# Part of the value projections of a hybrid decoder layer by Strassen's scheme, in one stage at the kernel's start

## The chip, the cores and the metric

The kernel runs on one core of a Trainium2 chip. The metric is the device time of one execution in microseconds: 1766.05 us before the change, the median of 3 runs (1765.07 to 1771.58). The profile is of one further execution, with the hardware's own record of what each engine did. PE is the matrix engine (TensorE), with its weight loads as PEld; DVE is the vector engine, ACT the scalar engine, POOL is GpSimd, and SP is the engine whose queue issues most of the DMAs.

## What is computed

One decoder layer on 1024 tokens of width 1024, all in fp32. Cut to what matters:

```python
h = rms_norm(x, pre_mix_g)                       # one scale per token, one gain per channel
proj = h @ w_in                                  # 8192 columns
qa, ka, va, qb, kb, vb, gates = split(proj)      # va: 512 columns, vb: 3 groups of 512
oa = diff_attention(rope(qa), rope(ka), va)      # 4 heads, causal, two softmaxes each
ob = merge of 3 dilated groups(rope(qb), rope(kb), vb)   # 4 heads per group
mix = (sigmoid(g_a) * (norm(oa) @ w_a_out) + sigmoid(g_b) * (ob @ w_b_out)) @ w_mix_out
x = x + rms_norm(mix);  x = x + rms_norm(conv_glu(rms_norm(x)))
```

The change touches `va` (512 columns) and the first group of `vb` (512 columns): two matrix products of the 1024 x 1024 normed input with 1024 x 512 weights.

## The kernel before

Every matrix product is made three times over. An fp32 operand is split into a high part, rounded to the format that PE multiplies in one pass, and a low part, the rest; a product is high x high + high x low + low x high (`mm3`, lines 146 to 149). A split (`split`, line 142) is one copy on ACT and one subtraction on DVE (lines 143 and 140). One PE matmul holds a 128 x 128 block still and streams up to 512 columns past it.

The input stands transposed in SBUF, as high and low parts `xh` and `xl`: 8 blocks of 128 channels, 1024 tokens each. The per-token norm factor `rstd` isn't in it. It is multiplied in behind each product: for values as a scale of the evacuation, for q and k through the rope tables, for gates through `rstd_row`. So products can start before the norm is known.

The stages, in order:

1. **First gates** (lines 318 to 376). The transposed input is loaded block by block, scaled by the gain and split; the first three gate units (128 columns each) run over it as the blocks arrive, on six PSUM banks. Behind that come the sums of squares of x (line 383), `rstd`, and the sine and cosine tables (`tables`, line 289), which are stored to DRAM and loaded in the layouts that the heads want (`load_tabs`).
2. **Start** (lines 674 to 676): `START_GATES` = 2 more gate units, the values of heads 0 and 1 of the first attention (`proj_v(VA, ...)`), the q and k of head 0 (`proj_a`).
3. **First attention**, heads 0 to 3. Each head has eight score blocks whose chain goes PE, DVE, ACT, DVE, PE, and beside them projections for later work as filler: `A_FILLS` (line 50) names them for each head. "p" and "P" are the q and k of the next head (8 units), "g" a gate (4 units), "v" and "w" the two halves of the values of heads 2 and 3 (4 units each), "V" the values of the second attention's group 0, first pair (8 units). A unit is 12 matmuls of 512 columns or 24 of 256. `interleave` (line 257) spreads them in step with the blocks.
4. **Second attention**, 12 steps of (pair, group, head), with the q and k of the next step (8 units) and half of the values of the next group (4 units) as filler (lines 862 to 873).
5. Output projections and the mixing matrix, then the gated MLP, whose two large products are already made by Strassen's scheme, with seven products of half-size blocks.

A values projection (`proj_v`, lines 429 to 466) covers 256 columns: it loads two weight units of 512 columns, splits them, and for each of eight token tiles runs 8 x 3 matmuls in which the input block is held and 256 weight columns stream (lines 438 to 440). Values of the first attention and of group 0 (dilation 1) go straight from PSUM to their split tiles (lines 448, 449). Those of dilated groups go through DRAM, where they are reordered (line 453).

The order of the program's text is not the order on the engines. A planner (line 1465) simulates all engines and places each instruction on its engine when its operands are ready, earlier text first; `tc.high_priority` moves some work ahead. What it decides is fixed in the program: each engine then runs its instructions in that order. Raw weights pass through `load_raw` (line 118), a two-buffer tag of the pool `rt`; split weights through six pairs of buffers (`slot_w`, line 114); PSUM has eight banks (`acc` 3, `pt` 2, `ps_s` 2, `ps_o` 1).

Of the kernel before, what the change touches and what calls it, by code (L numbers as in the profile page):

```python
# [24 lines left out]
P = 128  # L25
# [33 lines left out]
def plan():  # L59

    order = [("t", GT + i * P) for i in FIRST_GATES]
    for pair in range(2):
        for h in (2 * pair, 2 * pair + 1):
            order += [("t", QA + h * P), ("t", KA + h * P)]
            if h % 2 == 0:
                order += [("v", VA + pair * 256, i) for i in range(2)]
    for pair in range(2):
        for g in range(BG):
            order += [("v", VB + g * 512 + pair * 256, i) for i in range(2)]
            for h in (2 * pair, 2 * pair + 1):  # L70
                order += [("t", QB + g * 512 + h * P), ("t", KB + g * 512 + h * P)]
# [17 lines left out]
def trunk(ctx: ExitStack, tc: tile.TileContext, a, out):  # L89
# [28 lines left out]
    def load_raw(src):  # L118
        raw = raws_in[-1].tile([P, 512], F32, tag="raw", name="raw")
        dma(raw, src)  # L120
# [72 lines left out]
    v_d = dram.tile([4, S, 256], F32, name="v_d")  # L193
    gt_d = dram.tile([2 * KC, P, S], F32, name="gt_d")
# [82 lines left out]
    tabs = open_pool(attn, "tabs", side="right")  # L277
    rstd_row = tabs.tile([P, S], F32, name="rstd_row")
    slots = open_pool(attn, "slots", side="right")
    st_a = ExitStack()  # L280

# [7 lines left out]
    def tables(sin, cos, tmp):  # L289

        pos = tmp.tile([P, S], I32, tag="kk", name="pos")
        ang = tmp.tile([P, S], F32, tag="ang", name="ang")
        kk = tmp.tile([P, S], F32, tag="kk", name="kk")
        dma(pos, a["positions"].partition_broadcast(P))
        nc.vector.tensor_copy(ang, pos)
        nc.vector.tensor_scalar(ang, ang, cols[:, 0:1], None, op0=ALU.mult)
        for dst, off in ((sin, 0.0), (cos, 0.25)):
# [7 lines left out]
        nc.scalar.activation(sin, sin, AF.Sin)  # L305
        nc.scalar.activation(cos, cos, AF.Sin, bias=half_pi)
# [11 lines left out]
    with ExitStack() as st0:  # L318
        prep = open_pool(st0, "prep")
        ssx = prep.tile([P, 8], F32, name="ssx")  # L320
        raws = [prep.tile([P, 1024], F32, tag=f"raw{n}", name="raw") for n in range(len(FIRST_GATES))]
        first = [[Joined(t) for t in zip(*(slot_w() for _ in range(2)))] for _ in FIRST_GATES]
        xts = {}
# [9 lines left out]
        def load_x(k, parts=1):  # L333
            xts[k] = prep.tile([P, S], F32, tag="xt", name="xt", bufs=3)
# [10 lines left out]


# [9 lines left out]
        load_x(1)  # L356
        split_x(1)
# [3 lines left out]
        for k in range(2, KC):  # L361
            load_x(k)
            split_x(k)
        dma(cols, a["cols"])
# [3 lines left out]
        for k in range(KC):  # L368
            w = slice(k * P, (k + 1) * P)
            for n, ps in enumerate(pss):  # L370
                (wh, wl), sl = first[n // 2], halves()[n % 2]
                mm3(ps, wh[:, w], wl[:, w], xh[:, k, sl], xl[:, k, sl], k == 0, k == KC - 1)
# [5 lines left out]

        for m in range(8):
            t = prep.tile([P, D], F32, tag="xt", name="xn", bufs=3)  # L380
            dma(t, a["x"][m * P : (m + 1) * P, :])
            sq = prep.tile([P, D], F32, tag="kk", name="sq")
            nc.scalar.activation(sq, t, AF.Square, accum_out=ssx[:, m : m + 1])
        with tc.high_priority(offset=60):
            nc.vector.tensor_copy(rstd, rsqrt(ssx, D, prep, "rx"))
            spread = rstd_row.rearrange("p (m q) -> p m q", q=P)
            nc.vector.tensor_copy(spread, rstd.unsqueeze(2).to_broadcast([P, 8, P]))
        tab = [prep.tile([P, S], F32, tag="xt", name=n, bufs=3) for n in ("sin", "cos")]
        tables(*tab, prep)
        neg = prep.tile([P, S], F32, tag="xt", name="neg", bufs=3)  # L390
        for half, sl in enumerate(halves()):
            row = psum(F32, pt, "pt")
            for b in range(4):
                nc.tensor.transpose(row[:, b * P : (b + 1) * P], spread[:, half * 4 + b], ident)
            nc.scalar.activation(rstd_row[:, sl], row, AF.Copy)
# [1073 lines left out]
```

## Time and profile before

| | |
|---|---|
| median of 3 runs | 1766.05 us (1765.07 to 1771.58) |
| profiled execution: its time, its span | 1767.12 us, 1765.3 us |
| PE busy | 1721.8 us, 98% of the span, 8754 matmuls |
| DVE busy | 1329.9 us, 75% |
| ACT busy | 865.3 us, 49% |
| first gates end on PE, about | 43.4 us |
| start stage on PE: two gates, values, q and k of head 0 | 43.4 to about 118 us |
| mean granted clock of PE | 0.990 |

The span runs from the program's first instruction to its last. Busy time of an engine is the time in which at least one of its instructions is under way. The granted clock is the share of its full clock that PE was given. In a group of instructions the columns are line, engine, operation, what is written and read, shape and count, then busy us and the mean ns of one, then the engine's idle time just before them and what ended it. PE's matmuls overlap, so their mean is longer than the distance from one to the next.

### The profile page before, as it was taken

The page shows a single profiled execution, that of the slowest core. Times are in us where ns is not written, and L with a number is a line of the kernel's source. Part 1 is how long each engine was busy: PE and PEld are TensorE (multiplying, and loading weights), DVE is VectorE, ACT ScalarE, POOL GpSimd, SP SyncE. Part 2 cuts the span into 40 slices and gives each one's busy share as a digit, 9 for nine tenths or more (in the row PEclk, how much of TensorE's full clock was granted, in tenths as well). Part 3 has the DMA queues.
Part 4 walks back from the last instruction along what each step waited for, and adds up shares of the span by engine and source line. Part 5 has one row for each costly group of instructions (what it writes and reads, how often), then busy time and mean ns, then how long its engine had stood idle before and what let it go on. Part 6 is the DMA issues. An engine that isn't in the chain of part 4 may idle for free.

```text
span 1765.3 us, 24106 instructions
## 1 busy us (share of the span) xinstructions
PE 1721.8 (98%) x8754; PEld 1459.4 (83%) x8754; DVE 1329.9 (75%) x2612; ACT 865.3 (49%) x1585; POOL 51.6 (3%) x78
## 2 busy tenths in 40 slices
PE   9999999999999999999999999999999999999997
PEld 7987788789888888888877878878888888888886
DVE  4667786776556667565665867799999999789978
ACT  6375464644455645465652533364444444355452
POOL 0000000000000000000000410300000000000000
PEclk9999999999999999999999999999999999999999
DMA  8411112211121335221376533023222222196624
GB/s 271 162 60 42 54 55 72 78 55 59 56 86 60 102 97 156 75 88 55 126 254 222 166 131 108 37 72 107 90 78 95 78 78 96 60 342 216 206 77 155
DMA packets 100407, 197.61 MB, mean 112 GB/s; under 512 B 16368, under 2 KB 23216, under 8 KB 100288
## 3 DMA queue, kind: packets, MB, share of 16 engines
q1 hardware_dynamic: 92192, 185.06, 31.4%
q10 hardware_dynamic: 8096, 11.01, 1.7%
q8 instruction: 68, 1.11, 0.3%
q14 instruction: 51, 0.42, 0.1%
HBM read 152.37 MB, written 43.66 MB: 111 GB/s over the span
## 4 chain that ended last, share of the span: by engine, by line
PE 78%; DVE 9%; DMA 7%; issue 3%; ACT 3%; SPq 1%; POOL 0%; DVEq 0%; ACTq 0%
PE acc L148 15%; PE acc L147 15%; PE acc L149 15%; PE acc L438 3%; PE acc L440 3%; PE acc L439 3%; PE acc L1301 3%; PE acc L1300 3%; PE acc L1302 3%; PE acc L990 2%; PE acc L991 2%; PE acc L989 2%; PE o L484 2%; PE pt L472 1%; DMA og<-og_d 1%
## 5 line engine op out<-in xcount | busy, mean ns | idle before, releaser
L147 PE MATMUL acc<-xh,whi 128*128 128x512 f32 x744 | 296.3, 399 | 4.7 <-DVE t L421 2.6
L148 PE MATMUL acc<-xh,wlo 128*128 128x512 f32 x744 | 296.9, 399 | 1.4 <-DVE wlo L140 1.4
L149 PE MATMUL acc<-xl,whi 128*128 128x512 f32 x744 | 294.6, 398 | 0.0
L143 ACT ACTIVATE whi<-raw 128x512 fp32r<-128x512 f32 (+1 forms) x258 | 158.8, 624 | 208.5 <-PE acc L149 125.2
L140 DVE TENSOR_TENSOR wlo<-raw,whi 128x512 fp32r<-128x512 f32 (+1 forms) x255 | 185.0, 732 | 47.3 <-ACT whi L143 45.8
L147 PEld LDWEIGHTS acc<-xh,whi 128*128 128x128 f32 x744 | 140.6, 189 | 33.6 <-ACT xh L342 3.2
L148 PEld LDWEIGHTS acc<-xh,wlo 128*128 128x128 f32 x744 | 140.8, 189 | 29.2 <-DVE wlo L140 1.6
L149 PEld LDWEIGHTS acc<-xl,whi 128*128 128x128 f32 x744 | 141.2, 190 | 28.7
L147 PE MATMUL acc<-mh,whi 128*128 128x512 f32 x400 | 156.5, 391 | 1.9 <-ACT whi L143 1.7
L148 PE MATMUL acc<-mh,wlo 128*128 128x512 f32 x400 | 156.3, 391 | 0.2 <-DVE wlo L140 0.2
L149 PE MATMUL acc<-ml,whi 128*128 128x512 f32 x400 | 156.1, 391 | 0.0
L438 PE MATMUL acc<-whi,xh 128*128 128x256 f32 x512 | 147.4, 288 | 0.0
L440 PE MATMUL acc<-wlo,xh 128*128 128x256 f32 x512 | 146.8, 287 | 0.0
L439 PE MATMUL acc<-whi,xl 128*128 128x256 f32 x512 | 146.7, 287 | 0.0
L420 ACT ACTIVATE t<-acc 64x512 f32<-64x512 f32 (+1 forms) x160 | 94.6, 591 | 44.8 <-PE acc L149 42.4
L1175 DVE TENSOR_TENSOR u<-acc,u 128x512 f32<-128x512 f32 x133 | 90.6, 685 | 25.7 <-PE acc L149 25.6
L143 ACT ACTIVATE whi<-s 128x512 fp32r<-128x512 f32 x76 | 47.2, 628 | 105.2 <-PE acc L149 96.0
L439 PEld LDWEIGHTS acc<-whi,xl 128*128 128x128 f32 x512 | 97.7, 191 | 0.7
L438 PEld LDWEIGHTS acc<-whi,xh 128*128 128x128 f32 x512 | 97.8, 191 | 0.6
L440 PEld LDWEIGHTS acc<-wlo,xh 128*128 128x128 f32 x512 | 97.7, 191 | 0.5
L147 PEld LDWEIGHTS acc<-mh,whi 128*128 128x128 f32 x400 | 75.5, 189 | 18.2 <-ACT whi L143 2.1
L148 PEld LDWEIGHTS acc<-mh,wlo 128*128 128x128 f32 x400 | 75.5, 189 | 16.2 <-DVE wlo L140 0.5
(313 smaller groups left out, 3867.4 us busy)
## 6 DMA issues: line engine op xcount, KB each, us to landing
raw<-in_w_in SPq DMA_DIRECT2D x126, 256.0 KB, 2.7
raw<-in_w_up SPq DMA_DIRECT2D x88, 256.0 KB, 2.6
raw<-c_d SPq DMA_DIRECT2D x48, 256.0 KB, 3.5
c_d<-c SPq DMA_DIRECT2D x22, 512.0 KB, 2.7
raw<-in_w_down SPq DMA_DIRECT2D x37, 256.0 KB, 3.6
gl<-gt_d SPq DMA_DIRECT2D x16, 512.0 KB, 5.8
gt_d<-gate ACTq DMA_DIRECT2D x26, 256.0 KB, 2.0
og_d<-osb SPq DMA_DIRECT2D x12, 512.0 KB, 4.4
```

Source lines behind the costliest of these rows:

```text
L140: eng.tensor_tensor(lo, src, hi.bitcast(F32), op=ALU.subtract)
L143: nc.scalar.activation(hi, src, AF.Copy)
L147: nc.tensor.matmul(o, sh, mh, start=first, stop=False)
L148: nc.tensor.matmul(o, sl, mh, start=False, stop=False)
L149: nc.tensor.matmul(o, sh, ml, start=False, stop=last)
L420: nc.scalar.activation(t1[dst], ps[src], AF.Copy)
L438: nc.tensor.matmul(ps, xh[:, k, tk], wh[:, w], start=k == 0, stop=False)
L439: nc.tensor.matmul(ps, xl[:, k, tk], wh[:, w], start=False, stop=False)
L440: nc.tensor.matmul(ps, xh[:, k, tk], wl[:, w], start=False, stop=k == KC - 1)
L1175: nc.vector.tensor_tensor(to, made(p), x, op=ALU.add)
L1300: nc.tensor.matmul(banks[m], gh[:, tk], wh, start=f == 0, stop=False)
L1301: nc.tensor.matmul(banks[m], gl[:, tk], wh, start=False, stop=False)
```

## The change

The values of the first attention (512 columns) and of the second attention's group 0 (512 columns) are no longer projected by `proj_v` where they are wanted. One stage behind the first gates makes them all: their weights are laid side by side as a 1024 x 1024 matrix `w_v`, and the product with the 1024 x 1024 input is made as seven products of 512 x 512 blocks instead of eight. Each product is 4 contraction blocks x 4 token tiles x 3 matmuls of 512 columns, on one of two sets of four PSUM banks in turn.

- The four sums of the input's blocks that the scheme needs (T1 to T4) are made from the raw input while it arrives (`sums_x`), on ACT and DVE, and three of them are split and kept. -T1 is written over `xh` and `xl` of block row 1, tokens 512 to 1023, behind the first gates; during the fourth product that part of the input is loaded and split again.
- The input's blocks are loaded and contracted in the order 0, 4, 1, 5, 2, 6, 3, 7 (`K_FIRST`): all eight stay in SBUF (before: three buffers).
- The weights are loaded, summed on DVE where the scheme wants it, and split, five steps ahead of PE (`fetch_v`, `ready_v`). The products are added up in SBUF (`take_v`); finished blocks are scaled by `rstd` on ACT and stored to DRAM (`v0_d`) from ACT's queue.
- The sums of squares, the angles and the tables are placed between the products (`norm_x` at the second, `angles` at the third, `make_tables` at the fifth), in half-row loads that go round the three buffer tags `raw`, `t1` and `t2`.
- Where the attention wants these values, `values` loads them back from DRAM in four pieces and splits them. As filler that counts for nothing.
- One gate moves from the start (`START_GATES` 2 to 1) to head 3 (`"PVg"` to `"PVgg"`).
- Values of the dilated groups go through `proj_v` as they did.

```diff
-START_GATES, A_FILLS, B_GATES = 2, ("pggg", "pvgg", "wpgg", "PVg"), 3
+START_GATES, A_FILLS, B_GATES = 1, ("pggg", "pvgg", "wpgg", "PVgg"), 3
+K_FIRST = (0, 4, 1, 5, 2, 6, 3, 7)
...
+        def sums_x(k):
+            low, high = xts[k], xts[k + 4]
+            g1, g2 = gpre[:, k : k + 1], gpre[:, k + 4 : k + 5]
+            e, o = (tb.tile([P, 2, 512], F32, tag=t, name=t) for t in ("sin", "cos"))
+            nt1 = t1_raw[k // 2][:, k % 2]
+            def plus(out, x, g, y, op):
+                nc.vector.scalar_tensor_tensor(out, x, g, y, op0=ALU.mult, op1=op)
+            nc.scalar.activation(e[:, 0], low[:, 512:], AF.Copy, scale=g1)
+            plus(nt1, low[:, :512], g1, e[:, 0], ALU.subtract)
+            plus(e[:, 1], high[:, 512:], g2, e[:, 0], ALU.subtract)
+            split(t3[0][:, k], t3[1][:, k], e[:, 1])
+            plus(o[:, 0], high[:, 512:], g2, nt1, ALU.add)
+            split(t2[0][:, k], t2[1][:, k], o[:, 0])
+            plus(o[:, 1], high[:, :512], g2, o[:, 0], ALU.subtract)
+            split(t4[0][:, k], t4[1][:, k], o[:, 1])
...
-        for k in range(2, KC):
+        for n, k in enumerate(K_FIRST[2:], 2):
             load_x(k)
             split_x(k)
+            if n % 2:
+                sums_x(K_FIRST[n - 3])
+        sums_x(3)
...
+        order_v = (("p1", b11), ("p5", b12), ("p6", t2), ("p7", t3), ("p3", b22), ("p2", b21), ("p4", t4))
+        steps_v = [(p, x, k) for p, x in order_v for k in range(4)]
...
+        def ready_v(n):
+            p, _, k = steps_v[n]
+            raw = got_v.pop(n)
+            src = {"p1": wa[k], "p7": wa[k], "p5": wz[k], "p6": wz[k], "p3": wz[k]}.get(p) or raw[0]
+            if p == "p5":
+                tt(src, *raw, ALU.add)
+            if p == "p6":
+                tt(src, src, wa[k])
+            if p == "p7":
+                tt(src, src, raw[0])
+            if p == "p3":
+                tt(src, raw[0], src)
+            ready[n] = slot_w()
+            split(*ready[n], src)
+        def take_v(p, m, ps):
+            c11, c12, c21, c22 = (ys_v[q, m] for q in range(4))
+            if p == "p1":
+                nc.scalar.activation(c11, ps, AF.Copy)
+            if p == "p5":
+                nc.scalar.activation(c22, ps, AF.Copy)
+            if p == "p6":
+                tt(c21, ps, c11, ALU.add)
+                tt(c12, c21, c22, ALU.add)
+            if p == "p7":
+                tt(c21, ps, c21, ALU.add)
+                tt(c22, c21, c22, ALU.add)
+            if p in ("p3", "p2", "p4"):
+                to = {"p3": c12, "p2": c11, "p4": c21}[p]
+                tt(to, ps, to, ALU.add)
+            done = {"p7": (c22, 1, 1), "p3": (c12, 0, 1), "p2": (c11, 0, 0), "p4": (c21, 1, 0)}.get(p)
+            if done:
+                y, i, j = done
+                tk = j * 4 + m
+                nc.scalar.activation(y, y, AF.Copy, scale=rstd[:, tk : tk + 1])
+                nc.scalar.dma_start(v0_d[tk * P : (tk + 1) * P, i * 512 : (i + 1) * 512], y)
+        for k in range(4):
+            nt1 = t1_raw[k // 2][:, k % 2]
+            nc.scalar.activation(b12[0][:, k], nt1, AF.Copy, scale=-1.0)
+            nc.vector.scalar_tensor_tensor(b12[1][:, k], nt1, -1.0, f32(b12[0][:, k]), op0=ALU.mult, op1=ALU.subtract)
+        for n, (p, x, k) in enumerate(steps_v):
+            while fetched < min(n + 8, len(steps_v)):
+                fetch_v(fetched)
+                fetched += 1
+            while made < min(n + 5, len(steps_v)):
+                ready_v(made)
+                made += 1
+            if k == 0:
+                banks = ([psum() for _ in range(3)] + [psum(F32, ps_o, "o")] if n // 4 % 2 == 0 else
+                         [psum(F32, q, t) for q, t in ((ps_s, "s"), (pt, "pt")) for _ in range(2)])
+            if n == 4:
+                norm_x()
+            if n == 8:
+                pos = [load_raw(a["positions"][sl].partition_broadcast(P), next(tags)) for sl in halves()]
+                args = [tb.tile([P, S], F32, tag=n, name=n) for n in ("sin", "cos")]
+                angles(pos, *args, tb)
+            if n == 16:
+                make_tables([wv.tile([P, S], F32, tag=f"wz{i}", name="tab") for i in range(2)], *args)
+            wh, wl = ready.pop(n)
+            for m in range(4):
+                tk = slice(m * P, (m + 1) * P)
+                mm3(banks[m], x[0][:, k, tk], x[1][:, k, tk], wh, wl, k == 0, k == 3)
+            if k == 3:
+                for m in range(4):
+                    take_v(p, m, banks[m])
+            if p == "p7":
+                raw = load_raw(a["xT"][k][:, 512:], next(tags))
+                nc.scalar.activation(xh[:, k, 512:], raw, AF.Copy, scale=gpre[:, k : k + 1])
+                nc.vector.scalar_tensor_tensor(xl[:, k, 512:], raw, gpre[:, k : k + 1], f32(xh[:, k, 512:]), op0=ALU.mult,
+                                               op1=ALU.subtract)
...
+    def values(c, dil, res, pieces=range(4)):
+        n = S // dil // P
+        src = v0_d[:, c : c + 256].rearrange("(ih p r) c -> p r ih c", r=dil, ih=n)
+        for i in pieces:
+            if i % 2 == 0:
+                res.append(v_tiles(i // 2))
+            raw = load_raw(src[:, i * 2 // n, 2 * i % n : 2 * i % n + 2])
+            split(*(t.rearrange("p b c -> p (b c)")[:, i % 2 * 512 : (i % 2 + 1) * 512] for t in res[-1]), raw)
+            yield 0
...
-        run(proj_v(VA, vs[0]))
+        run(values(0, 1, vs[0]))
...
-                "v": lambda: (proj_v(VA + 256, vs[1], ms=range(4)), 4),
-                "w": lambda: (proj_v(VA + 256, vs[1], ms=range(4, 8)), 4),
+                "v": lambda: (values(256, 1, vs[1], range(2)), 0),
+                "w": lambda: (values(256, 1, vs[1], range(2, 4)), 0),
...
-                "V": lambda: (values_of(0, 0), 8),
+                "V": lambda: (values_of(0, 0), 0),
```

More of the change, by code (lines that the diff above doesn't have):

```diff
@@ L377, in trunk @@
             dma(gt_d[i], t)
[L379 to L395, printed above, removed]
-            nc.vector.scalar_tensor_tensor(neg[:, sl], tab[0][:, sl], -1.0, row, op0=ALU.mult, op1=ALU.mult)
-            nc.vector.tensor_tensor(tab[0][:, sl], tab[0][:, sl], row, op=ALU.mult)
-            nc.vector.tensor_tensor(tab[1][:, sl], tab[1][:, sl], row, op=ALU.mult)
-        for t, to in zip((tab[1], tab[0], neg), tab_d):
-            dma(to, t)
-        cos_a, sin_a = load_tabs(64, 32)
         lv = prep.tile([P, 4 * QK], F32, name="lv")
@@ L413, in trunk, with norm_x @@
         nc.vector.tensor_scalar(nlam, nlam, -LAM_INIT, None, op0=ALU.add)
+    def norm_x():
+        ssx = tiny.tile([P, 2, 8], F32, name="ssx", bufs=1)
+        for m in range(8):
+            for half, sl in enumerate(halves()):
+                t = load_raw(a["x"][m * P : (m + 1) * P, sl], next(tags))
+                nc.scalar.activation(t, t, AF.Square, accum_out=ssx[:, half, m : m + 1])
+        tt(ssx[:, 0], ssx[:, 0], ssx[:, 1], ALU.add)
+        nc.vector.tensor_copy(rstd, rsqrt(ssx[:, 0], D, tb, "rx"))
```

160 lines of the change are left out of this document (97 added, 63 removed).

## The prediction

> **What bounds the kernel now.** I read the page's busy times and chain first, then busy time by stretch of time, then single groups. Page, parts 1 and 4:
>
> ```profile
> span 1765.3 us, 24106 instructions
> ...
> PE 1721.8 (98%) x8754; PEld 1459.4 (83%) x8754; DVE 1329.9 (75%) x2612; ACT 865.3 (49%) x1585; POOL 51.6 (3%) x78
> ...
> PE 78%; DVE 9%; DMA 7%; issue 3%; ACT 3%; SPq 1%; POOL 0%; DVEq 0%; ACTq 0%
> ```
>
> TensorE (PE) is busy for 98% of the span and makes 78% of the chain that ended last. So a change pays if it shortens PE's stream and opens no holes in it. The stretches that it touches (columns: length, then busy us and instruction count of PE, PEld, DVE, ACT, POOL, then granted clock, DMA share, GB/s):
>
> ```profile
> 43.40:65.25 21.85, 21.85 (x103) 18.13 (x102) 19.17 (x37) 7.70 (x12) 0.82 (x2) 1.00 0.52 168
> 65.25:88.28 23.03, 23.03 (x194) 23.03 (x192) 10.90 (x19) 6.49 (x12) 0.00 (x0) 1.00 0.45 151
> ```
>
> The first stretch is the two START gates, 2 x 48 = 96 matmuls 512 wide: 21.85/96 = 0.2276 us each. The second is the values projection of heads 0 and 1, alone on PE: 192 matmuls 256 wide in 23.03 us, 0.1199 us each, a little over half the price of the wide ones. PE is full in both. The group's count, over the whole span:
>
> ```profile
> L438 PE MATMUL acc<-whi,xh 128*128 128x256 f32 x512 | 147.4, 288 | 0.0
> ```
>
> 512 on each of three lines are 1536 = 8 values projections of 192. (The mean of 288 ns overlaps its neighbours and isn't the price.)
>
> **The change part by part.** *Removed.* Four of the eight projections: two of the first attention, two of the second's group 0. 4 x 23.03 = 92.1 us of PE. In place: one before head 0, half of one in head 1, half in head 2, one in head 3, one over the two steps of group 2 in the second attention's first pair.
>
> *Added.* Seven products x 4 contraction blocks x 4 token tiles x 3 = 336 matmuls 512 wide: 336 x 0.2276 = 76.5 us. PE's stream gets 92.1 - 76.5 = **15.6 us shorter**. The count is fixed by the program and both prices are of full stretches, so this term is firm.
>
> *Where it must be won.* The new stage stands where 23.0 us of values and one gate (48 x 0.2276 = 10.9 us) stood, so the start grows by 76.5 - 23.0 - 10.9 = 42.6 us. It is given back in heads 1 to 3 (11.5 + 11.5 + 23.0 - 10.9, the gate now being in head 3 = 35.1 us) and in two later steps (23.0 us). That holds only as far as those stretches are bound by PE.
>
> *The vector engine in the new stage.* DVE's new work, in operations on 512 columns: 28 for the sums of x (four calls of seven), 4 for -T1, 28 for splitting weights, 16 for sums of weights, 24 adds out of PSUM before the last product ends (8, 8, 4, 4), 4 to restore the overwritten half of x: 104. What stays is what it does up to 88.28 us now, 19.24 + 19.17 + 10.90 = 49.3 us, less what goes or moves behind the stage (8 evacuations at 0.482, 12 splits and gate evacuations at 0.682: 12.0 us), 37.3 us.
>
> ```profile
> L449 DVE SCALAR_TENSOR_TENSOR vl<-acc,edge,vh 128x256 fp32r<-128x256 f32 x8 | 3.9, 482 | 11.6 <-ACT vh L448 11.6
> ```
>
> ```profile
> 0.00:42.00 42.00, 38.70 (x152) 30.97 (x153) 19.24 (x27) 24.50 (x37) 4.09 (x9) 0.96 0.84 275
> ...
> 1600.00:1640.00 40.00, 40.00 (x178) 33.10 (x178) 40.00 (x67) 19.84 (x34) 0.00 (x0) 1.00 0.68 226
> ```
>
> ```profile
> L1246 DVE TENSOR_TENSOR ax<-ax,raw 128x512 f32<-128x512 f32 x11 | 7.5, 682 | 0.0
> ```
>
> ```profile
> 3.98 0.42 DVE L140 TENSOR_TENSOR wlo<-raw,whi 128x256 fp32r<-128x256 f32 x1 [2.82 <-ACT whi L143]
> ...
> 1600.32 0.68 DVE L140 TENSOR_TENSOR wlo<-az,whi 128x512 fp32r<-128x512 f32 x1
> 1600.92 0.68 DVE L140 TENSOR_TENSOR wlo<-by,whi 128x512 fp32r<-128x512 f32 x1
> ```
>
> An operation lasts 0.682 us, yet the next one starts 0.60 us after it: in the down-projection's stage 67 fit into 40.00 us, 0.597 each, and there PE is full (40.00 of 40.00) beside a DVE that is full too. That stage is made the same way as the new one, so it is the nearest row. The work that has to be done before PE may go past its 21st of 28 steps is 104 x 0.682 + 37.3 less the last 14 operations (six splits, eight adds, 9.5 us) = 98.7 us by durations; by starts it is 90 x 0.597 + 37.3 = 91.0 (the 37.3 is busy time, in which overlaps count once already). DVE's first operation is at 4 us and I allow it 4 more for waits on x; seven steps of 12 x 0.2276 us follow, 19.1 us. The stage would end at 8 + 98.7 + 19.1 = 125.8 or at 8 + 91.0 + 19.1 = 118.1 us, against 43.4 + 76.5 = 119.9 by PE alone. So the delay lies between 5.9 us and nothing, with 1.8 us to spare; I take nothing, by the row in which both engines are full.
>
> The Trainium skill speaks against that: "VectorE: DVE Perf Modes", section on the TRN2 errata, has a 512-column fp32 tensor_tensor at 691 ns with the read latency exposed between instructions, so 67 would need 46.3 us. The duration agrees with 0.682 us, the spacing of 0.597 does not, and I go by the spacing; the other is a rival below.
>
> *Seams of the new stage.* What the trace does not show: the planner's order of gate evacuation, -T1 and the first splits at 43.4 us, and some 13 us of angle work on DVE in the middle of the third product (six of the first kind below, and shorter ones). Bounds: 0 (the down-projection's stage) to one evacuation, negation and split queue, 11 x 0.60 = 6.6 us. I take 2, a third.
>
> ```profile
> L300 DVE SCALAR_TENSOR_TENSOR cos<-kk,ang 128x1024 f32<-128x1024 f32 x1 | 1.2, 1225 | 0.0
> ```
>
> ```profile
> L383 ACT ACTIVATE sq<-xn 128x1024 f32<-128x1024 f32 x8 | 8.5, 1057 | 5.9 <-DMA xn<-in_x 5.6
> ```
>
> ```profile
> L143 ACT ACTIVATE whi<-raw 128x512 fp32r<-128x512 f32 (+1 forms) x258 | 158.8, 624 | 208.5 <-PE acc L149 125.2
> ...
> raw<-in_w_in SPq DMA_DIRECT2D x126, 256.0 KB, 2.7
> ...
> gt_d<-gate ACTq DMA_DIRECT2D x26, 256.0 KB, 2.0
> ```
>
> ScalarE has room: 28 splits, 24 evacuations and scalings and 8 copies at 0.62, the squares (8.5 us, and more in halves: 12 at most), tables and 16 store issues are some 60 of 76 us. DMA: 28 weight tiles, 16 of x, 4 reloaded and 16 stored, of 256 KB, are 16.8 MB in 76.5 us, 219 GB/s, as in the row at 1600 us (226). On SyncE's queue the values' loads for head 0 wait for the last product's stores; queued behind are the weights of head 0's projection, which PE wants only after the gate, 10.9 us later. That covers a store and a load (2.0 + 2.7 us); uncovered it would cost those 4.7 us.
>
> *Heads 1 to 3 with less to fill.* Each had 20 units of projection (a unit is 12 wide matmuls, 2.7 us) beside its softmax chain and gets 16.
>
> ```profile
> 200.00:265.00 65.00, 65.00 (x376) 57.00 (x375) 54.28 (x154) 42.05 (x84) 0.00 (x0) 1.00 0.17 53
> 265.00:345.00 80.00, 78.56 (x438) 68.22 (x436) 58.34 (x168) 43.80 (x89) 0.00 (x0) 0.98 0.20 63
> 345.00:430.00 85.00, 83.33 (x514) 74.56 (x513) 65.30 (x185) 40.00 (x84) 1.59 (x4) 1.00 0.18 58
> ...
> 160.00:190.00 30.00, 22.40 (x110) 17.66 (x109) 23.06 (x91) 15.79 (x40) 0.00 (x0) 0.83 0.03 11
> ```
>
> ```profile
> 221.00:241.00 20.00, 20.00 (x123) 17.90 (x122) 18.89 (x46) 16.27 (x33) 0.00 (x0) 1.00 0.13 41
> ```
>
> PE is idle for 3.1 of these 230 us, DVE busy for 177.9. Without the projections DVE loses 16 evacuations (7.7 us) and 12 splits (8.2) and gets 8 splits and a gate (8.2): 170.2 in 195 us, 87%. At 221 us DVE is busy for 94% beside a full PE, so throughput isn't the limit; latency can be, as at 160 us in head 0, where PE stands idle for 7.6 us and the clock falls to 0.83. Bounds: -5 (a new plan that closes such a hole) to 3 x 11.4 = 34 us (the 160 us stretch in each head: 7.6 idle, and 22.4 x 0.17 = 3.8 lost to the clock). I take +3, nearer to the 221 us row, which is of these heads.
>
> *The two later steps.* They keep the 8 units of the next projection and lose 4. The step that has none of these today:
>
> ```profile
> 848.00:882.00 34.00, 34.00 (x171) 28.01 (x170) 23.47 (x58) 21.91 (x43) 0.00 (x0) 1.00 0.44 139
> ```
>
> PE is full there, so I take 0; the bound above is 1 us each, below 0.
>
> *Off the path.* The contraction order, the larger x buffers, the two arrival tags and the table code moved behind the sums change what waits at 6 to 43 us, where PE's own 144 matmuls (32.8 us) fill most of it; 0, bounds -2 to +2.
>
> **Sum.** -15.6 + 0 (DVE) + 2 (seams) + 3 (heads) + 0 = **-10.6 us**. The profiled execution took 1767.1 us, 1.8 of them around its span; it would take 1756.5. The runs' median, 1766.05, is 1.1 below that execution, so the forecast is 1755.5, rounded to **1756 us**, its own range 1750 to 1760.
>
> **The rivals.** *DVE sets the new stage* (26%). By durations the stage ends 5.9 us late: -10.6 + 5.9 = -4.7, 1761 us. For it: 98.7 us of work in a stretch with almost no slack, and orders that wait for ScalarE in between. Against it: the full rows at 1600 us. This is the way that the errata rule of the Trainium skill, quoted above, would have it.
>
> *The heads can't use the time* (17%, slower). With 4 of 20 units gone, the softmax chain (scores, maximum, exponential, transposes) ends last in heads 1 to 3 and PE waits as at 160 us: 34 us in place of 3, -15.6 + 2 + 34 = +20, 1786 us; with two thirds of that in each head, 1775. It decides from (15.6 - 2)/3 = 4.5 us a head. For it: head 0, with all 20 units, has such a hole. Against it: heads 1 to 3 have 3.1 us in all. The Trainium skill, "TensorE: Matmul & The Clock Gate", Part 1, says that an idle window of some 3.4 us halves the clock; the 0.83 at 160 us agrees, and without it the hole would be 7.6 us.
>
> *The new plan closes old holes as well* (10%). The 11.4 us around 160 us go, and the heads lose nothing: -15.6 + 2 - 11.4 = -25, 1741 us. Nothing in the edit aims at head 0; only the other order speaks for it.
>
> That the arithmetic isn't shortened can be left out, since the matmuls are counted.
>
> **How the numbers follow.** The forecast gets 47%. A measurement of this kernel tells apart about 0.5%, 8.8 us, so faster means under 1757.2 and slower over 1774.9. Faster: the 10% and some 34 of the 47 (its centre lies close to the bound) = 0.44. Slower: 15 of the 17%, since the slow rival at less than two thirds of its price stays under 1774.9 = 0.15. The same: the rest, 0.41. The range has to hold the forecast, the DVE rival and the lower part of the slow one: 1747 to 1777 us, with some 8% below and 10% above.
>
> **What would show it.** PE with 8754 - 768 + 336 = 8322 matmuls, the 256-wide groups with 256 on each line. The new stage from the end of the first gates to its last product: 77 to 80 us if I am right, 82 and more if DVE sets it, with waits of PE for the low halves of weights or for PSUM adds. In heads 1 to 3, PE idle for under 7 us and a clock above 0.96; a clock below that, and transposes waiting for the subtraction of the two softmaxes, would make me wrong on the slow side. The later steps of group 2 some 11 us shorter each with PE full.

## The result and the profile after

The changed kernel takes 1822.74 us, the median of 4 runs (1820.97 to 1824.04). The kernel before, run beside it, takes 1767.82 us (1765.07 to 1771.58). The ratio is 1.0309, with a 95% interval of 1.0285 to 1.0332: the change makes the kernel 3.1% slower, some 55 us. The forecast was 1756 us, so some 67 us are to be explained. The profiled execution took 1822.28 us.

Parts 1 and 2 of the page of the changed kernel (part 2 has 40 slices of 45.5 us; the digits are tenths of busy time and of granted clock):

```profile
span 1820.5 us, 23499 instructions
...
PE 1740.9 (96%) x8322; PEld 1440.6 (79%) x8322; DVE 1375.4 (76%) x2686; ACT 895.8 (49%) x1641; POOL 51.6 (3%) x78
...
PE   8898989998999997999999999999999999999997
...
PEclk9999989999899998999999999999999999999999
```

The matmuls are the forecast 8322, 432 fewer than before. Yet PE is busy for 19 us longer than before, and on top of that it is idle for some 36 us more (1820.5 - 1740.9 = 79.6, before 43.5). So two things went wrong: there are holes, and what is left of the stream runs slower, in part because the granted clock falls too (mean 0.977, before 0.990). Before, every digit of PE but the last was 9. The eights and the seven show where the holes are: around the new stage (slices 2 and 4; the first slice ends at its entry), in the first attention (6 and 10) and in one place of the second (16).

Busy time by stretch (columns: the stretch, its length, then busy us and instruction count of PE, PEld, DVE, ACT, POOL, then granted clock, DMA share, GB/s), in the changed kernel:

```profile
51.60:131.20 79.60, 79.58 (x345) 65.52 (x346) 63.36 (x110) 46.78 (x92) 1.30 (x2) 0.97 0.59 203
...
215.00:262.00 47.00, 38.58 (x188) 31.46 (x187) 33.34 (x115) 18.42 (x45) 0.00 (x0) 0.89 0.11 40
262.00:330.00 68.00, 65.10 (x328) 54.67 (x328) 55.81 (x159) 41.80 (x84) 0.00 (x0) 0.97 0.17 58
330.00:400.00 70.00, 66.11 (x324) 55.77 (x323) 55.30 (x165) 41.27 (x83) 0.00 (x0) 0.95 0.22 65
400.00:470.00 70.00, 60.23 (x294) 49.90 (x293) 52.03 (x161) 31.48 (x68) 1.17 (x4) 0.88 0.14 48
...
665.00:740.00 75.00, 60.94 (x282) 49.55 (x281) 51.04 (x132) 39.14 (x88) 0.00 (x0) 0.89 0.39 122
740.00:900.00 160.00, 160.00 (x995) 142.21 (x994) 97.43 (x209) 88.42 (x188) 0.00 (x0) 1.00 0.28 94
```

Between its first and its last product the new stage (first row) is close to what the prediction made it: 79.6 us, PE full from end to end. Counted as the prediction counts it, from the end of the first gates at 44.31 us, it is 86.9 us, with the wait at its entry. The rest of the loss is outside of it. In the heads, 215 to 470 us, PE is idle for 25.0 of 255 us and the clock falls to 0.88; at 665 to 740 us, where the prediction had a full PE, it is idle for 14.1 us. Not all of the 25.0 us is new: the row at 215 us lies mostly in head 0, whose score products begin at 180 us here and at 118 us before, and the prediction's row at 160 us shows that hole in the kernel before (7.6 us idle, clock 0.83).

**The entry of the new stage.** SyncE's queue in the changed kernel (start us, length us, operation, count), and then PE at the same place:

```profile
43.34 2.76 SPq L413 DMA_DIRECT2D gt_d<-gate  x3
46.16 2.40 SPq L474 DMA_DIRECT2D wa<-in_w_v  x4
```

```profile
43.92 0.39 PE L151 MATMUL o<-xl,whi 128*128 128x512 f32 x1
51.62 0.79 PE L149 MATMUL acc<-whi,xh 128*128 128x512 f32 x1 [7.31 <-ACT whi L145]
52.21 0.63 PE L150 MATMUL acc<-whi,xl 128*128 128x512 f32 x1
52.64 0.63 PE L149 MATMUL acc<-whi,xh 128*128 128x512 f32 x1
53.06 0.63 PE L150 MATMUL acc<-whi,xl 128*128 128x512 f32 x1
```

The stage's first weights `wa` are issued only behind the three stores of the gates, and those wait for the gates to be evacuated from PSUM. PE stands for 7.31 us. After that its matmuls start 0.43 us apart, not 0.2276: the clock has been halved (the granted clock is 0.50 from 51.6 to 56.0 us). This agrees with the Trainium skill, "TensorE: Matmul & The Clock Gate", Part 1, by which an idle window halves the clock and 512 columns then take 426.7 ns.

**Its exit.** The chain of waits of the changed kernel between 129 and 148 us (start, length, what):

```profile
130.08 2.08 DMA v_d<-yv
...
132.28 3.99 DMA raw<-v_d
...
136.35 3.38 DMA v_d<-yv
...
139.75 0.64 ACT vh L145
...
140.42 0.70 DVE vl L142
...
141.14 2.67 DMA raw<-v_d
...
145.27 2.62 DMA raw<-in_w_in
```

The last products are stored, loaded into the two `raw` buffers, split, and only then is a weight of head 0's projection loaded into the freed `raw`. PE waits 6.4 us from 142.2 us on. The gate in front of it (10.9 us) didn't cover this.

**In the heads.** SyncE's queue between 205 and 302 us, and the splits of `raw` on ACT there (with the first and last start):

```profile
210.25 2.22 SPq L122 DMA_DIRECT2D raw<-in_w_in  x2
219.42 6.31 SPq L122 DMA_DIRECT2D raw<-v_d  x2
254.01 40.69 SPq L768 DMA_DIRECT2D oa_d<-osb  x2
300.26 0.93 SPq L122 DMA_DIRECT2D raw<-in_w_in  x2
```

```profile
L145 ACT ACTIVATE vh<-raw x2: 612/621/630, 297.2 to 297.8; 128x512 fp32r<-128x512 f32 x2
```

Two loads of values are issued at 219.4 to 225.7 us; they fill both `raw` buffers. They are split at 297.2 us, some 72 us later. In between no weight is loaded: the next one goes out at 300.26 us, right after the splits. So PE runs short of other work for the softmax chain's gaps; whether that makes the holes is asked by e_direct below. This repeats in the same form at 376.9 us (weights again at 462.9) and, in the second attention, at 651.6 us (weights again at 684.8) and 693.2 us (722.7).

**Where there is no hole.** The up projection, 1240 to 1480 us, first before and then after the change:

```profile
1240.00:1480.00 240.00, 240.00 (x1061) 198.72 (x1060) 221.91 (x294) 104.09 (x141) 2.58 (x26) 1.00 0.25 85
```

```profile
1240.00:1480.00 240.00, 240.00 (x1030) 192.32 (x1030) 219.31 (x297) 102.24 (x141) 2.41 (x24) 1.00 0.25 88
```

PE is full and its clock is 1.00 in both, and in the same 240 us it starts 1061 matmuls before and 1030 after: 226 ns and 233 ns each. The change touches nothing in this stage. But it takes a 64-byte tile (`ssx`) from a pool that lies ahead of the weights' buffers. In the compiled kernels the weights `whi` and `wlo` begin, in each partition, at 128 modulo 256 bytes before the change and at 192 after, while the moving operand of the up projection (`mh`, `t2h` and the like) is at 128 in both. The input `xh` and `xl` moves along with the weights, to 192, so the gates and the q and k projections keep equal places.

### The profile page after: what moved, and what is told of

Read it like the earlier page. It is cut to its first block, busy times and chain, and to the rows that moved or that the text cites. A ratio compares the mean times of both kernels' runs of the same rounds, so it can differ in the third digit from the quotient of the medians.

```text
span 1820.5 us, 23499 instructions
## 1 busy us (share of the span) xinstructions
PE 1740.9 (96%) x8322; PEld 1440.6 (79%) x8322; DVE 1375.4 (76%) x2686; ACT 895.8 (49%) x1641; POOL 51.6 (3%) x78
## 4 chain that ended last, share of the span: by engine, by line
PE 77%; DVE 8%; DMA 8%; ACT 4%; issue 2%; SPq 0%; POOL 0%; ACTq 0%; DVEq 0%; POOLq 0%
PE acc L149 16%; PE acc L150 16%; PE acc L151 16%; PE acc L1443 3%; PE acc L1445 3%; PE acc L1444 3%; PE acc L593 2%; PE acc L595 2%; PE acc L594 2%; PE acc L1137 1%; PE acc L1135 1%; PE o L630 1%; PE acc L1136 1%; PE pt L618 1%; DVE wlo L142 1%
## 5 line engine op out<-in xcount | busy, mean ns | idle before, releaser
L145 ACT ACTIVATE whi<-raw 128x512 fp32r<-128x512 f32 (+1 forms) x246 | 151.6, 624 | 227.6 <-PE acc L151 105.3
L142 DVE TENSOR_TENSOR wlo<-raw,whi 128x512 fp32r<-128x512 f32 (+1 forms) x243 | 175.3, 727 | 64.1 <-ACT whi L145 61.3
L151 PEld LDWEIGHTS acc<-ml,whi 128*128 128x128 f32 x400 | 74.9, 187 | 18.3
L1444 PE MATMUL acc<-whi,wlo 128*128 128x512 f32 x220 | 77.6, 390 | 0.0
L576 DVE TENSOR_TENSOR t<-acc,cos 128x512 f32<-128x512 f32 x64 | 44.1, 690 | 43.6 <-ACT t L575 43.2
L1443 PE MATMUL acc<-whi 128*128 128x512 f32 x220 | 76.3, 391 | 0.0
L630 PE MATMUL o<-pt,vh 128*128 128x512 f32 (+1 forms) x188 | 62.4, 382 | 12.4 <-DVE pt L142 6.7
L593 PE MATMUL acc<-whi,xh 128*128 128x256 f32 x256 | 73.8, 288 | 0.0
```

The lines of the kernel that those rows point to most:

```text
L142: eng.tensor_tensor(lo, src, hi.bitcast(F32), op=ALU.subtract)
L145: nc.scalar.activation(hi, src, AF.Copy)
L151: nc.tensor.matmul(o, sh, ml, start=False, stop=last)
L593: nc.tensor.matmul(ps, xh[:, k, tk], wh[:, w], start=k == 0, stop=False)
L630: nc.tensor.matmul(o[:, :, q0 : q1 + 1], vs[b // 4][0][:, b % 4, c], t, start=first and n == 0, stop=False)
L1443: nc.tensor.matmul(banks[m], gh[:, tk], wh, start=f == 0, stop=False)
```

## The experiments

Theory, from the profile: of the 67 us, some 35 are the held `raw` buffers, some 13 the 64-byte shift, and some 14 the two seams. The rival from the prediction: the heads lost too much fill, and the softmax chain ends last whatever the weights do. "Against after" below is the difference of two ratios to the kernel before, times 1768 us.

| kernel | median us | ratio to before, 95% interval | against after, us |
|---|---|---|---|
| after | 1822.74 | 1.0309 [1.0285, 1.0332] | |
| e_direct | 1796.36 | 1.0151 [1.0125, 1.0178] | -28 |
| e_phase | 1809.60 | 1.0226 [1.0203, 1.0248] | -15 |
| e_seam1 | 1819.62 | 1.0274 [1.0253, 1.0295] | -6 |
| e_seam2 | 1824.52 | 1.0308 [1.0283, 1.0332] | 0 |
| e_all | 1776.60 | 1.0051 [1.0033, 1.0070] | -46 |
| e_three | 1779.47 | 1.0052 [1.0032, 1.0071] | -45 |
| e_fill0 | 1770.71 | 1.0002 [0.9988, 1.0016] | -54 |
| e_fill1 | 1765.98 | 0.9966 [0.9954, 0.9979] | -61 |
| e_fill3 | 1764.38 | 0.9965 [0.9950, 0.9980] | -61 |
| e_fill4 | 1774.41 | 1.0030 [1.0020, 1.0040] | -49 |
| e_shift (of before) | 1787.84 | 1.0113 [1.0097, 1.0128] | |
| e_both (of before) | 1774.15 | 1.0029 [1.0017, 1.0040] | |

### e_direct: the values no longer pass through raw

```diff
-            raw = load_raw(src[:, i * 2 // n, 2 * i % n : 2 * i % n + 2])
-            split(*(t.rearrange("p b c -> p (b c)")[:, i % 2 * 512 : (i % 2 + 1) * 512] for t in res[-1]), raw)
+            h, l = (t[:, i % 2 * 2 : i % 2 * 2 + 2] for t in res[-1])
+            dma(f32(l), src[:, i * 2 // n, 2 * i % n : 2 * i % n + 2])
+            split(h, l, f32(l))
```

> The changed kernel, but the value loads of later use are written straight into the place of their low part (tile vl) and split there, so that they take none of the two buffers raw of the weights. Theory (the loads of the values hold both raw buffers until vh and vl of the group before come free, 72 to 80 us each time, and no weight load of the next head can start, so that TensorE has nothing to put into the softmax chain's gaps): weight loads go on between 220 and 300 us and between 377 and 457 us, TensorE's windows at 215-262, 400-470 and 665-740 us fill again, and the kernel is 25 to 45 us shorter than the changed one, 1778 to 1798 us. Rival (the heads lost too much filler to the new stage, so the chain of score, maximum, exponent and transpose ends last whatever the weights do): under 5 us, 1818 to 1823 us, with the same waits of pt and s.

Measured: 1796.36 us, 28 us less. SyncE's queue in this kernel:

```profile
144.02 72.40 SPq L122 DMA_DIRECT2D raw<-in_w_in  x14
245.00 0.33 SPq L769 DMA_DIRECT2D oa_d<-osb  x1
254.24 21.93 SPq L122 DMA_DIRECT2D raw<-in_w_in  x4
285.01 0.33 SPq L769 DMA_DIRECT2D oa_d<-osb  x1
286.01 0.33 SPq L122 DMA_DIRECT2D raw<-in_w_in  x1
286.43 0.90 SPq L567 DMA_DIRECT2D vl<-v_d  x2
```

Weights go on between 254 and 286 us, and the value loads themselves now leave at 286.43 us. So their places are free only then; in the changed kernel the loads ran 67 us ahead of that and held what the weights needed. Its stretches at the end of the first attention and in the second:

```profile
400.00:470.00 70.00, 65.10 (x320) 53.63 (x319) 51.04 (x151) 32.02 (x69) 1.17 (x4) 0.95 0.18 61
...
640.00:740.00 100.00, 95.78 (x530) 81.97 (x529) 73.44 (x175) 57.76 (x128) 0.00 (x0) 0.98 0.47 146
```

PE is idle for 4.2 us at 640 to 740 us, where it had 14.1 us between 665 and 740 alone. At the new stage's exit it waits 0.5 us instead of 6.4. At 400 to 470 us it is idle for 4.9 us instead of 9.8. These three make 20.7 of the 28 us, and the mean granted clock rises from 0.977 to 0.984 as well. The hold is the largest single cause.

The first stretch that was expected to fill did not, though:

```profile
215.00:262.00 47.00, 38.42 (x182) 31.23 (x181) 34.51 (x121) 18.59 (x44) 0.00 (x0) 0.89 0.12 45
```

PE is idle for 8.6 us there, as in the changed kernel (8.4). For the most part that is head 0's old hole, and taking the hold away doesn't change it.

What this edit doesn't give back is PE's wait for the subtraction of the two softmaxes. The groups of waits of PE over the whole span (us in total, times, longest), in the kernel before, in after and in e_direct:

```profile
PE pt L472 <- DVE s L556: 4.3, 2, 2.8
```

```profile
PE pt L618 <- DVE s L702: 9.2, 5, 2.8
```

```profile
PE pt L619 <- DVE s L703: 9.0, 6, 2.8
```

That part is the rival's, and it is taken up below.

### e_phase, e_shift, e_both: the 64 bytes

e_phase is the changed kernel with one tile taken from another pool:

```diff
-        ssx = tiny.tile([P, 2, 8], F32, name="ssx", bufs=1)
+        ssx = tb.tile([P, 2, 8], F32, name="ssx")
```

> The changed kernel, but the 64-byte tile of the first sums of squares is taken from another pool, so that the weights' tiles lie at the addresses modulo 128 that they had before. Theory (the 64-byte tile moves whi and wlo from phase 0 to phase 64 of 128 bytes, while mh and ml stay at phase 0, and a matmul whose two operands differ in phase is spaced some 6 ns wider): the 512-wide matmuls of the up projection go back from 233 to 227 ns and the kernel is 10 to 16 us shorter than the changed one, 1807 to 1813 us. Rival (the wider spacing comes from other traffic in that stage): no change, 233 ns, 1820 to 1825 us.

e_shift is the kernel before with nothing but an unused tile of 64 bytes and a fill of it:

```diff
     tiny = open_pool(ctx, "tiny", bufs=4)
+    nc.vector.memset(tiny.tile([P, 16], F32, name="shift", bufs=1), 0.0)
```

> The kernel before, with one more tile of 64 bytes ahead of the others (and one small fill of it), so that the weights' tiles lie 64 bytes further than they did. Nothing else of the change is in it. Theory (a phase of 64 of 128 bytes between the weights and the moving operand widens the spacing): the up projection's matmuls go from 227 to 233 ns and the kernel is 8 to 16 us longer than before, 1775 to 1784 us. Rival (the phase has no part in it): within 3 us of before, 1765 to 1771 us.

e_both is e_shift, and 192 unused bytes on the other side, ahead of the moving operands:

```diff
-    edge = open_pool(ctx, "edge", side="right").tile([P, 24], F32, name="edge")
+    edge = open_pool(ctx, "edge", side="right").tile([P, 72], F32, name="edge")
```

> The kernel before, with the 64-byte tile ahead of the weights' tiles and, on the other side of the memory, 192 unused bytes more ahead of the moving operands' tiles, so that all of them lie at 64 of 128 bytes and, as in the kernel before, at the same place of 256. Theory (what counts is that the two operands of a matmul have the same phase): the up projection's matmuls are back at 227 ns and the time is that of the kernel before, 1763 to 1773 us. Rival (a tile that doesn't begin at a multiple of 128 bytes is read more slowly, whatever the other operand does): 233 ns, 1783 to 1792 us.

Measured: e_phase 15 us less than after; e_shift 20 us more than before (1.0113), more than was expected; e_both 5 us more than before (1.0029), just above the expected range. PE's 8322 matmuls stand in the same order in after and in e_phase. e_shift and e_both share one order too, which differs from that of the kernel before in 51 of 8754 places. The up projection's stretch in e_shift, in e_both and in e_phase:

```profile
1240.00:1480.00 240.00, 240.00 (x1031) 193.70 (x1030) 215.97 (x286) 100.12 (x135) 2.58 (x26) 1.00 0.25 84
```

```profile
1240.00:1480.00 240.00, 240.00 (x1060) 198.74 (x1059) 221.49 (x294) 104.07 (x140) 2.49 (x25) 1.00 0.25 85
```

```profile
1240.00:1480.00 240.00, 240.00 (x1061) 198.75 (x1059) 224.67 (x303) 105.62 (x143) 2.48 (x25) 1.00 0.26 87
```

Weights at 192 and the moving operand at 128 modulo 256 (after, e_shift): 1030 and 1031 matmuls. Both at 128 (before, e_phase) or both at 192 (e_both): 1060 and 1061. So it isn't that a tile begins off a multiple of 128 bytes: the two operands of a matmul have to agree. The 5 us that remain in e_both aren't in this stretch: in the profiled executions of e_shift and of e_both alike, PE's 400th matmul starts some 3 us later than before and its 4000th 7 to 8 us later. So they belong to the tile or to the changed order and not to the two operands' places; their cause was not looked for. What the places cost is e_shift less e_both, 15 us or 0.8%, the same as in e_phase.

### e_seam1, e_seam2, e_three: the new stage's ends

e_seam1 stores the first gates from ScalarE's queue:

```diff
-            dma(gt_d[i], t)
+            nc.scalar.dma_start(gt_d[i], t)
```

> The changed kernel, but the stores of the gates go out on ScalarE's queue in place of SyncE's. Theory (the first weights of the values' stage stand in SyncE's queue behind three gate stores that wait for the gates' evacuation, and TensorE waits 7.3 us for them at 44 us): that idle falls to under 2 us and the kernel is 4 to 10 us shorter, 1812 to 1818 us. Rival (the weights' place in memory is freed only by the last sum of squares at 45.6 us): the idle stays at about 7 us, 1820 to 1825 us.

Measured: 6 us less, with intervals that overlap after's; the time lies 2 us above the expected range. The waits of PE at 35 to 70 us, first after, then e_seam1 (us in total, times, longest):

```profile
PE acc L149 <- ACT whi L145: 7.3, 1, 7.3
```

```profile
PE acc L149 <- ACT whi L145: 2.5, 1, 2.5
```

4.8 us of the idle time are gone, as the queue's theory has it; 2.5 us stay, where under 2 were expected. A little of it comes back at once: PE now waits for the token norms and tables in the stage, 1.0 and 1.2 us.

e_seam2 writes head 0's projection ahead of the first values:

```diff
-        run(values(0, 1, vs[0]))
         run(proj_a(0, ops[0]))
+        run(values(0, 1, vs[0]))
```

> The changed kernel, but the projection of head 0 is written before the loads of the first group's values. Theory (the projection's weights stand in SyncE's queue and in the two raw buffers behind value loads that wait for the stores of the new stage's last product; TensorE waits 6.4 us for them at 142 us): that idle falls to under 2 us, and the kernel is 4 to 9 us shorter, 1813 to 1818 us. Rival (what the projection gains is lost again because the values come later than the first head's product with them needs): TensorE waits as long a little later, 1820 to 1825 us.

Measured: no change. The waits of PE up to 215 us in e_seam2:

```profile
PE s L684 <- ACT k L658: 8.0, 2, 6.9
```

The projection no longer waits, but behind it PE stands for k. SyncE's queue in e_seam2 says why:

```profile
138.75 32.59 SPq L122 DMA_DIRECT2D raw<-v_d  x4
176.94 1.43 SPq L122 DMA_DIRECT2D raw<-in_w_in  x2
```

The value loads hold `raw` a little later instead, from 138.75 us on, and no weight of head 1 is loaded before 176.94 us. So there is no fill while the last q and k pass through the rotation on ACT and DVE, and PE waits for them. The wait was only moved. e_three asks this the other way: it has e_direct, e_phase and e_seam1, but the order of after.

> The four edits without the fourth: the first values are loaded ahead of head 0's projection, as in the changed kernel. Theory (the 6.4 us that TensorE waits behind the first gate come from raw buffers that value loads hold while the products' stores are under way, and the loads straight into the values' tiles take this cause away): within 3 us of the four edits, 1774 to 1780 us. Rival (the cause is the order in SyncE's queue, in which the projection's loads stand behind the value loads that wait for the stores): 5 to 9 us longer, 1781 to 1786 us.

Measured: 1.0052, beside 1.0051 with the new order (e_all). With the values out of `raw` the order makes no difference: the exit seam was the hold once more.

### e_all: the four edits together

> The changed kernel with four edits at once: the values' loads go straight into their own tiles, the sums' tile is taken from another pool, the gates' stores go out on ScalarE's queue, and head 0's projection is written ahead of the first values. Theory (the loss is the sum of the held raw buffers, some 35 us, the phase, some 13 us, and the two seams, some 14 us; they add up): 1750 to 1770 us, some 60 us shorter than the changed kernel. Rival (the fourteen of the fifteen microseconds that the removed products give are lost in the heads because filler is missing there, and the four add up to less than half): above 1790 us.

Measured: 1776.60 us, 46 us less than after. The single edits give 28 + 15 + 6 + 0 = 49, so they add up nearly; but the time lies above the range that was expected, and the kernel is still 0.5% slower than before, although PE's stream is 15.6 us shorter. Some 25 us are still lost.

### e_fill0, e_fill1, e_fill3, e_fill4: fill for the heads

Only the constants that place the free gates differ from e_all. In order: e_all, e_fill1, e_fill0, e_fill3, e_fill4.

```diff
-START_GATES, A_FILLS, B_GATES = 1, ("pggg", "pvgg", "wpgg", "PVgg"), 3
+START_GATES, A_FILLS, B_GATES = 1, ("pggg", "pvggg", "wpgg", "PVgg"), 2
+START_GATES, A_FILLS, B_GATES = 0, ("pggg", "pvggg", "wpgg", "PVgg"), 3
+START_GATES, A_FILLS, B_GATES = 0, ("pggg", "pvggg", "wpggg", "PVgg"), 2
+START_GATES, A_FILLS, B_GATES = 1, ("pggg", "pvggg", "wpggg", "PVgg"), 1
```

> The kernel with the four edits, and one gate's projection (48 products, 10.9 us of TensorE) moved from the last step of the second attention into the fill of head 1. Theory (the nine microseconds that are left over the kernel before are lost in the heads, where TensorE waits in the softmax chain because the values' products are no longer there to fill it: some 7 us at 280 to 320 us): 3 to 7 us shorter than the four edits alone, 1769 to 1774 us. Rival (head 1 is bound by VectorE and ScalarE, and each gate in it makes it longer by its whole time; or the last step waits as much more): 0 to 6 us longer, 1777 to 1783 us.

> The kernel with the four edits, and the one gate that stands between the values' stage and head 0 moved into the fill of head 1. Theory (head 1 lacks fill): 3 to 8 us shorter than the four edits alone, 1768 to 1774 us, less whatever the gate covered. Rival (the gate covers the loads of head 0's weights and tables, and without it TensorE waits some 4.7 us there): no gain, 1774 to 1781 us.

> Both moves, and the two gates go to head 1 and to head 2. Theory (both heads lack fill): 6 to 12 us shorter than the four edits alone, 1764 to 1771 us, about as long as the kernel before. Rival: 1775 to 1785 us.

> The kernel with the four edits, one gate before head 0 as in the changed kernel, and two of the three gates of the second attention's last step moved to heads 1 and 2. Theory (heads 1 and 2 lack fill, and the last step needs at most one gate): at most 1766 us, 1757 to 1766 us. Rival (the last step of the second attention needs two gates to fill it, and with one TensorE waits there as much as the heads gain): 1767 to 1775 us.

The first three were run side by side with e_three (1779.47 us): e_fill1 takes 13.5 us less, e_fill0 8.8, e_fill3 15.1, each more than was expected. One gate out of the last step gives most of it; the second, out of the start, adds less than the runs of one kernel differ. A gate is 10.9 us of PE wherever it stands, so what is gained is idle time and clock. The heads, 260 to 480 us, in e_three and then in e_fill3:

```profile
260.00:480.00 220.00, 209.10 (x1030) 173.07 (x1029) 167.97 (x495) 117.61 (x238) 1.17 (x4) 0.97 0.21 66
```

```profile
260.00:480.00 220.00, 214.31 (x1067) 179.38 (x1067) 165.21 (x475) 112.25 (x230) 1.16 (x4) 0.98 0.23 74
```

37 more matmuls, 8 us of PE, fit into the same 220 us, though DVE and ACT do no more work. PE's idle time there falls from 10.9 to 5.7 us. So the heads were short of fill, and not bound by the other engines. These 8 us are about half of the 15; the rest lies outside of this stretch and was not taken apart. e_fill3 is 0.35% faster than the kernel before (0.2 to 0.5 by the interval), the best that was found, with e_fill1 as good; that is 6 of the 15.6 us. In e_fill4 the last step of the second attention has one gate left; its stretch and e_fill3's:

```profile
880.00:1030.00 150.00, 138.99 (x621) 111.86 (x619) 109.05 (x193) 83.00 (x138) 21.04 (x16) 0.96 0.61 205
```

```profile
880.00:1030.00 150.00, 142.90 (x646) 115.40 (x645) 110.40 (x183) 74.50 (x124) 24.56 (x18) 1.00 0.65 222
```

25 matmuls fewer and a clock of 0.96: that step needs two gates, and what one more gate would give the heads is lost there, as the rival had it.

## Why the prediction was wrong

- **PE's stream, -15.6 us: right as a count.** 8322 matmuls, and a new stage of 79.6 us against 76.5 plus 2.2 for the half-clock start (4.4 us at 0.50). Wrong was the silent assumption behind it, that 0.2276 us per matmul holds for all the rest. It became 0.233 in the up projection, because 64 bytes were put ahead of the weights. The prediction's part "off the path: 0, -2 to +2" named the larger buffers and the moved code, but not the place of every other tile. It measured 15 us (e_phase), and in the kernel before 15 of the 20 us of e_shift (e_shift less e_both).
- **DVE in the new stage, 0: a little low, and not tested by the changed kernel.** PE has no gap in the stage there, but it enters it 7.3 us late, more than the 5.9 us that the rival by durations would cost. Where the entry costs only 2.5 us, PE does wait for what DVE makes. PE's waits in e_all, up to 215 us, hold these three (us in total, times, longest):

```profile
PE pt L446 <- DVE rstd_row L441: 1.7, 1, 1.7
PE acc L149 <- DVE yv L295: 1.5, 1, 1.5
PE pt L149 <- DVE tab L450: 1.3, 1, 1.3
```

  The first and the third are in the stage, 3.0 us together (2.2 in e_seam1); the second is right behind it, for a PSUM bank that DVE's adds still read. So the total alone doesn't refute the rival. The spacing does speak for the prediction's price: in the changed kernel DVE is busy for all of 85 to 115 us, and its 512-column operations start 0.60 us apart there too (three adds from 94.38 us, the next operation at 96.18).
- **Seams of the new stage, +2 of 0 to 6.6: mis-sized, and partly misplaced.** PE waits 7.3 us at the entry and 6.4 at the exit. At the entry the prediction looked at DVE's queue; what stood in the way was SyncE's, with stores that wait ahead of the first weights (e_seam1: 4.8 us of idle time). At the exit it named the value loads that wait for stores, but took them for an order in a queue, with a gate as cover. They hold the two `raw` buffers as well, and another order only moves the wait (e_seam2).
- **Heads 1 to 3, +3: wrong, by a mechanism that it didn't have.** It counted the fill that was left and asked whether the softmax chain could stand it. It did not ask whether that fill could be loaded: values that come through DRAM take a `raw` buffer when they are loaded and give it back only when their own places are free, 72 us later. Together with the second attention and the exit that made 28 us (e_direct); how much of it is the heads' alone was not separated. The slow rival (34 us, the softmax chain) had the sign and the wrong main cause; its cause is there too, at a smaller size. e_three, which is rid of the other causes, is still 9 us longer than before where the stream is 15.6 shorter, 25 in all, and moving one gate recovers 13.5 of them (e_fill1), two 15 (e_fill3). How much of these 15 the change itself took, and how much the kernel before could also have won by moving gates, was not measured. The prediction's remark on the idle window is borne out only in part: in its own row at 160 us the longest idle time of PE is 2.8 us, and the granted clock is 0.50 from 169.8 to 176.7 us, so less idle time than that window was enough.
- **Two later steps, 0: wrong.** 14.1 us of idle time at 665 to 740 us, by the same hold; 4.2 us at 640 to 740 without it. The row at 848 us, a step without value projections and with PE full, was a good witness for the fill but not for the buffers, since it has no value load.
- The remaining 9 or so of those 25 us are, as far as is known, the entry's last 2.5 us, the waits in the new stage, and places that no run took apart.

## What to carry to other kernels

When a product moves from "made where it is used" to "made early, stored, loaded again", cost the buffer that its reload lands in, from the load to the moment its last reader is done; if that is a buffer that weights also pass through, a load that runs ahead stops them. Fill that is taken out of a latency-bound stage has to be replaced, or part of what the shorter stream gains is spent on waiting. And before reading a difference of stages that a change doesn't touch as noise, count the instructions in a full stretch of both: 1061 against 1030 in the same 240 us found the 64 bytes.

## What was not expected of the hardware

In the up projection, matmuls of 512 fp32 columns with a weight load each start 226 ns apart when the weights and the moving operand begin at the same place modulo 256 bytes in their partitions, and 233 ns apart when these differ by 64; the granted clock is 1.00 in both. It was seen at the phases 128/128 and 192/192 against 192/128 only. With the roles changed the price is smaller: in the changed kernel's new stage, where the sums T2 to T4 (at 128) are held and the weights (at 192) stream, 15 matmuls start between 127.75 and 130.96 us, 229 ns apart on average. Whether a difference of 32 or 128 bytes does the same, and which read of the memory is delayed, no run here shows. The Trainium skill, "SBUF — State Buffer", section "Operand start alignment", gives the multiple of the element size at which an operand may start, and says that this is about legality and not speed; this is a case for the speed.
